# Fewer rows in the software stores of one chunk: two constants in a kernel that the DMA engines bound

## The chip, the cores and the metric

The kernel runs on one core of a Trainium2 chip. The metric is the device time of an execution in microseconds (us); each quoted time is a median over several executions. Before and changed kernel are compared on the same chip in alternating rounds. "Span" is the time from the first to the last recorded instruction of one profiled execution; it is 1.3 to 1.8 us shorter than the device time of the same execution.

## The reference

```python
# x: [16, 2048, 256] float32, W: [256, 256], lora_A: [256, 16], lora_B: [16, 256], lora_E: [16]
x_flat = x.reshape(-1, in_dim)                       # 32768 x 256
y = x_flat @ W
lora_out = ((x_flat @ lora_A) * lora_E) @ lora_B
y = y + scale * lora_out                             # back to [16, 2048, 256], float32
```

Input and output are 33.5 MB each, and all of it has to go through the DMA engines once.

## The kernel before

The 32,768 rows are cut into 4 chunks, each 128 partitions x 64 rows x 1 KB. A chunk is loaded into one of three buffers ("homes"), computed in place, and stored from there. For each group of four rows of all partitions GpSimd casts to bf16, TensorE transposes, VectorE copies back, TensorE multiplies with one merged weight, and ScalarE writes the result over the input. The order of the loads ("L") and stores ("S") of the hardware queue, as (chunk, first row, end row):

```python
ORDER = [
    ("A",), ("L", 0, 0, 16), ...          # cut: the other loads of chunks 0 to 2
    ("S", 0, 0, 40), ("S", 0, 40, 64),
    ("L", 3, 0, 32), ("L", 3, 32, 64),
    ("S", 1, 0, 64),
    ("S", 2, 2, 62),
    ("S", 3, 0, 64),
]
SHARED = 2
END_ROWS = 2
SHARES = (slice(108, 113), slice(0, 108), slice(113, P))
```

Of chunk 2 the hardware queue stores rows 2 to 61. GpSimd stores rows 0, 1, 62 and 63 with three software DMAs, one for each slice of the partitions:

```python
def share(engine, p, landed):
    def ends_of(rows):
        return rows[p].rearrange("p (q b) k -> p q b k", b=END_ROWS)[:, :: ROWS // END_ROWS - 1, :, :]
    engine.dma_start(out=ends_of(y_chunks[SHARED]), in_=ends_of(home(SHARED))).then_inc(landed, 16)

# GpSimd, after its last cast:
gpsimd.wait_ge(s_turned, N_GROUPS - NS + 1)
gpsimd.drain().then_inc(s_stage[N_GROUPS % UNROLL], 1)
gpsimd.wait_ge(s_shared, 1)
for p in SHARES:
    share(gpsimd, p, shared_stored)

# the hardware queue's engine, after its last issue:
sync.wait_ge(shared_stored, 16 * len(SHARES))
...                                        # cut: closing steps, then a wait for the last hardware stores
```

Of the kernel before, what the change touches and what calls it, by code (L numbers as in the profile page):

```python
# [27 lines left out]
    ("L", 3, 0, 32),  # L28
    ("L", 3, 32, 64),
    ("S", 1, 0, 64),  # L30
    ("S", 2, 2, 62),
    ("S", 3, 0, 64),
]

SHARED = 2
END_ROWS = 2
SHARES = (slice(108, 113), slice(0, 108), slice(113, P))

HELD = (2, 0)
# [18 lines left out]
def kernel(  # L58
# [105 lines left out]
# [4 lines that stand above are left out]
# [177 lines left out]
```

## Time and profile before

| | before |
|---|---|
| time, median of 6 executions | 161.32 us (161.14 to 161.55) |
| span of the profiled execution | 159.8 us |
| bytes moved | 67.43 MB, 422 GB/s over the span |
| busiest compute engine | PE, 60% |
| wait for the software stores over | 154.9 us |

How to read it: the prediction below shows the lines for the bound (the queues' share of sixteen engines), the stages and the queue's waits. Here is only the chain of work that ended last in the kernel before, by line, as a share of the span:

```profile
DMA out_dram<-home 28%; PE psum_y L269 25%; PE psum_xt L258 14%; DMA home<-in_x_dram 5%; POOL stage L200 1%; ACT home L221 1%; PE psum_y L291 1%; SPq L147 0%; ACTq L225 0%
```

PE (TensorE) stands in this chain with 40%, though it is not the bound: the chain ends with the issue of the last store, which waits for the last group. When that store is issued, at 122.4 us, the hardware queue still has some 16 us of chunks 1 and 2 ahead of it, so an earlier end of the compute should have moved nothing. A chain tells what released what; whether the queue in front of it was empty has to be read from the DMA share.

### The profile page before, as it was taken

What the parts mean: (1) busy time and instruction counts of PE and PEld (TensorE: products, weight loads), DVE (VectorE), ACT (ScalarE), POOL (GpSimd) and SP (SyncE); (2) the same over time, 40 slices, a digit from 0 to 9 for tenths busy, and PEclk for the clock granted to TensorE, in tenths of its full rate; (3) what the DMA queues carried; (4) which work ended last, traced back from release to release, by engine and by line L of the source; (5) the groups of instructions that cost most, each with busy time, mean ns of one, the idle gap of its engine ahead of it and who ended that gap; (6) DMA issues with size and microseconds to landing.
All of it is one profiled execution on the core that took longest, in us unless ns stands there. A gap on an engine that the chain in (4) does not pass through costs nothing.

```text
span 159.8 us, 2074 instructions
## 1 busy us (share of the span) xinstructions
PE 96.1 (60%) x782; PEld 84.2 (53%) x782; DVE 45.4 (28%) x66; ACT 66.1 (41%) x65; POOL 69.3 (43%) x73
## 2 busy tenths in 40 slices
PE   2769999999999900000999999999993000000000
PEld 1246899999999900000799999999992000000000
DVE  0113355555555500000155555555550000000000
ACT  3001477777777720000267777777775000000000
POOL 1072577777787300002577777778762000000000
PEclk9999999999999995555599999999999555555555
DMA  7999999999979997989999999998998997989976
GB/s 271 427 455 431 400 453 443 476 394 402 583 328 525 410 377 328 468 359 441 406 482 402 435 468 402 509 443 377 492 434 355 481 486 306 545 345 480 491 312 263
DMA packets 2451, 67.43 MB, mean 422 GB/s; under 512 B 512, under 2 KB 528, under 8 KB 784
## 3 DMA queue, kind: packets, MB, share of 16 engines
q1 hardware_dynamic: 2016, 66.60, 97.4%
q0 software_dynamic: 224, 0.52, 0.9%
q10 hardware_dynamic: 208, 0.28, 0.6%
q14 instruction: 3, 0.02, 0.0%
HBM read 33.85 MB, written 33.55 MB: 422 GB/s over the span
## 4 chain that ended last, share of the span: by engine, by line
PE 40%; DMA 33%; POOL 1%; ACT 1%; issue 0%; SPq 0%; ACTq 0%
DMA out_dram<-home 28%; PE psum_y L269 25%; PE psum_xt L258 14%; DMA home<-in_x_dram 5%; POOL stage L200 1%; ACT home L221 1%; PE psum_y L291 1%; SPq L147 0%; ACTq L225 0%
## 5 line engine op out<-in xcount | busy, mean ns | idle before, releaser
L200 POOL CAST stage<-home 128x1024 bf16<-128x1024 f32 x64 | 66.6, 1042 | 48.2 <-PE psum_xt L258 21.7
L221 ACT COPY home<-psum_y 128x1024 f32<-128x1024 f32 x64 | 64.8, 1012 | 54.3 <-PE psum_y L269 54.3
L269 PE MATMUL psum_y<-weff,xt 128*128 128x256 bf16 x512 | 69.0, 280 | 0.0
L242 DVE COPY xt<-psum_xt 128x1024 bf16<-128x1024 bf16 x64 | 44.3, 691 | 65.8 <-PE psum_xt L258 65.8
L258 PE MATMUL psum_xt<-ident,stage 128*128 128x128 f32 x260 | 41.9, 286 | 22.3 <-POOL stage L200 22.3
L269 PEld LDWEIGHTS psum_y<-weff,xt 128*128 128x128 bf16 x512 | 51.4, 100 | 6.2
L258 PEld LDWEIGHTS psum_xt<-ident,stage 128*128 128x128 f32 x260 | 32.3, 148 | 24.9 <-issue 23.7
L282 PE MATMUL psum_y<-ident 128*128 128x512 f32 x4 | 3.8, 1100 | 2.9 <-POOL ident L180 2.9
L282 PEld LDWEIGHTS psum_y<-ident 128*128 128x128 f32 x4 | 1.2, 323 | 3.9 <-POOL ident L180 2.9
L230 DVE TENSOR_SCALAR ate<-psum_y,e_sb 16x256 f32<-16x256 f32 x1 | 0.5, 472 | 7.2 <-DMA e_sb<-in_lora_E_dram 7.2
L168 POOL DMA_DIRECT2D out_dram<-home x3 | 2.0, 675 | 1.0 <-PE psum_xt L258 1.0
L221 ACT ACT_TABLE_LOAD x1 | 1.3, 1283 | 2.1 <-SPq L304 2.1
L291 PE MATMUL psum_y<-b_sb,ate 16*128 16x256 f32 x4 | 2.1, 666 | 0.0
L291 PEld LDWEIGHTS psum_y<-b_sb,ate 16*128 16x128 f32 x4 | 1.2, 318 | 0.5 <-issue 0.3
L246 DVE TENSOR_TENSOR weff<-w_sb,psum_y 128x512 bf16<-128x512 f32 x1 | 0.7, 687 | 1.4 <-PE psum_y L291 1.4
L178 POOL MEMSET ident<- 128x128 f32 x1 | 0.2, 205 | 1.7 <-SPq L304 1.7
L285 PEld LDWEIGHTS psum_y<-ident,a_sb 128*16 128x16 f32 x2 | 0.3, 137 | 1.2 <-issue 1.2
L285 PE MATMUL psum_y<-ident,a_sb 128*16 128x128 f32 x2 | 0.6, 421 | 0.0
L180 POOL TENSOR_SCALAR_AFFINE_SELECT ident<-ident 128x128 f32<-128x128 f32 x1 | 0.3, 283 | 0.2 <-POOL ident L178 0.2
L326 POOL MEMSET const-float32-0.0<- 128x1 f32 x1 | 0.1, 93 | 0.2 <-issue 0.2
L326 POOL MEMSET const-bfloat16-1.0<- 128x1 bf16 x1 | 0.1, 96 | 0.0
L326 POOL MEMSET const-uint8-127<- 128x1 uint8 x1 | 0.1, 96 | 0.0
(1 smaller groups left out, 0.1 us busy)
## 6 DMA issues: line engine op xcount, KB each, us to landing
home<-in_x_dram SPq DMA_DIRECT2D x4, 4096.0 KB, 24.4
out_dram<-home SPq DMA_DIRECT2D x1, 7680.0 KB, 38.2
home<-in_x_dram SPq DMA_DIRECT2D x2, 3072.0 KB, 16.7
out_dram<-home SPq DMA_DIRECT2D x1, 5120.0 KB, 45.2
out_dram<-home SPq DMA_DIRECT2D x1, 3072.0 KB, 44.7
home<-in_x_dram SPq DMA_DIRECT2D x1, 2048.0 KB, 7.6
out_dram<-home POOLq DMA_DIRECT2D x1, 432.0 KB, 30.2
w_sb<-in_W_dram ACTq DMA_DIRECT2D x1, 256.0 KB, 2.8
```

The costliest lines, as they stand in the source:

```text
L168: engine.dma_start(out=ends_of(y_chunks[SHARED]), in_=ends_of(home(SHARED))).then_inc(landed, 16)
L200: gpsimd.tensor_copy(out=stage[g % NS][:], in_=home(c)[:, b:b + CG, :]).then_inc(s_stage[g % UNROLL], 1)
L221: scalar.copy(out=home(c)[:, b:b + CG, :], in_=psum_y[g % NY][:]).then_inc(s_free[(g + NY) % UNROLL], 1)
L230: vector.tensor_scalar(out=ate[:], in0=psum_y[0][:R, :KT, :P], scalar1=e_sb[:], scalar2=float(scale), op0=ALU.mult, op1=ALU.mult,).then_in ...
L242: vector.tensor_copy(out=xt[g % NX][:], in_=psum_xt[g % NT][:].bitcast(BF16)).then_inc(s_xt[g % UNROLL], 1)
L246: vector.tensor_add(out=weff[:], in0=w_sb[:], in1=psum_y[1][:, :KT, :]).then_inc(s_free[0], 1)
L258: ins = tensor.transpose(psum_xt[i % NT][:, b, :], words[:, b, :], ident[:])
L269: ins = tensor.matmul(psum_y[i % NY][:, b, :], xt[i % NX][:, b, t::KT], weff[:, t, :], start=(t == 0), stop=(t == KT - 1),)
L282: tensor.matmul(psum_y[1][:, :2, :], ident[:], ident[:, None, :].to_broadcast([P, 4, P]), start=True, stop=True)
L285: ins = tensor.transpose(psum_y[0][:R, t, :P], a_sb[:, t, :], ident[:])
L291: ins = tensor.matmul(psum_y[1][:, t, :], ate[:, t, :], b_sb[:], start=True, stop=True)
L326: nc = _bacc.Bacc("TRN2", target_bir_lowering=False, num_devices=1)
```

## The change

The intent is to give less work to the software stores: one row at either end of chunk 2 in place of two, and the rows between to the hardware store. The whole diff:

```diff
-    ("S", 2, 2, 62),
+    ("S", 2, 1, 63),
     ("S", 3, 0, 64),
 ]
 
 SHARED = 2
-END_ROWS = 2
+END_ROWS = 1
```

The title under which the change was handed over also names straight code and drains (the prediction refers to it); they are not in the diff.

## The prediction

> **What bounds the kernel now.** I read the page first: the engines' busy shares, the forty slices, the DMA queues and the chain that ended last.
>
> ```profile
> PE 96.1 (60%) x782; PEld 84.2 (53%) x782; DVE 45.4 (28%) x66; ACT 66.1 (41%) x65; POOL 69.3 (43%) x73
> ...
> PE   2769999999999900000999999999993000000000
> ...
> DMA  7999999999979997989999999998998997989976
> ...
> DMA packets 2451, 67.43 MB, mean 422 GB/s; under 512 B 512, under 2 KB 528, under 8 KB 784
> ...
> q1 hardware_dynamic: 2016, 66.60, 97.4%
> q0 software_dynamic: 224, 0.52, 0.9%
> q10 hardware_dynamic: 208, 0.28, 0.6%
> ```
>
> No compute engine is busy over 60% of the span, and PE is empty in the last nine slices. The 16 DMA engines are full nearly throughout: the packets of queues q1, q0 and q10 take 97.4 + 0.9 + 0.6 = 98.9% of sixteen engines' span. So the bound is the packet time of the DMA engines. The software stores that the change is about are q0: 0.52 MB.
>
> Next, the stages. The columns are length, then busy time of PE, PEld, DVE, ACT and POOL, granted clock, DMA share, GB/s:
>
> ```profile
> 100.00:122.00 22.00, 21.32 (x196) 19.59 (x193) 10.59 (x16) 16.93 (x18) 16.17 (x17) 1.00 1.02 441
> 122.00:135.00 13.00, 0.00 (x0) 0.00 (x0) 0.00 (x0) 0.37 (x1) 0.00 (x0) 0.58 1.03 443
> 135.00:150.00 15.00, 0.00 (x0) 0.00 (x0) 0.00 (x0) 0.00 (x0) 0.00 (x0) 0.50 1.01 435
> 150.00:158.50 8.50, 0.00 (x0) 0.00 (x0) 0.00 (x0) 0.00 (x0) 0.00 (x0) 0.50 0.88 377
> 158.50:159.80 1.30, 0.00 (x0) 0.00 (x0) 0.00 (x0) 0.00 (x0) 0.00 (x0) 0.50 0.01 0
> ```
>
> From 122 us on only stores run, at 435 to 443 GB/s with every engine full; the last engines drain between 158.5 and 159.4 us. The end is therefore the end of whichever DMA engine has the longest list of packets. Last, the queue's own waits, the issues, and the instruction that follows the wait for the software stores:
>
> ```profile
> SPq L147 <- DMA out_dram<-home: 32.1, 1, 32.1
> ...
> out_dram<-home SPq DMA_DIRECT2D x1, 7680.0 KB, 38.2
> ...
> out_dram<-home POOLq DMA_DIRECT2D x1, 432.0 KB, 30.2
> ...
> out_dram<-home POOLq DMA_DIRECT2D x1, 60.0 KB, 34.8
> ...
> out_dram<-home POOLq DMA_DIRECT2D x1, 20.0 KB, 9.5
> ...
> L147 SPq COMPARE_BRANCH  x1: 33/33/33, 154.9 to 154.9; - x1
> ```
>
> The wait for the software stores is over by 154.9 us, more than 4 us before the end. They take the engines' time but their completion does not hold the end. They are 20 + 432 + 60 = 512 KB for 5 + 108 + 15 = 128 partitions: 4 KB each, 2 KB at either end.
>
> **Engine by engine.** No view prints the engine of a packet, but the trace has every packet's start, duration, size and queue, and on a full engine the next packet begins within about 4 ns of the last one's end. Matching ends to starts from 112 us on gives 16 lists. Twelve have 10 software packets of 4,096 B; four have 2 each, and in the other 8 turns an 8 B dummy of 9 ns. (At one place two lists run together, and which one holds a 539 ns packet is my choice: I give it to the list that would otherwise have only one.) Durations, from these records: 65,536 B 2,418 ns; 61,440 B (chunk 2's store) 2,267 ns; 4,096 B 159 ns; 2,048 B (the load of W) 84 ns; 1,024 B 46 ns. Per KB it is (2,418 - 2,267) / 4 = 38 ns. The lists end, in us:
>
> - the twelve: 158.46, 158.57, 158.64, 158.70, 158.71, 158.81, 158.81, 158.82, 158.98, 159.02, 159.02, 159.03
> - the four: 158.65, 158.97, 159.08, 159.39
>
> So the uneven shares are a balance: at 113 us the four were behind the twelve (their packets begin at 112.97 to 113.58, those of the twelve at 112.20 to 112.76), and 8 x (159 - 9) = 1,200 ns less work lets them almost catch up. Almost: one of the four still ends last.
>
> **What the Trainium skill says.** "DMA: Bandwidth & Descriptors", section "Queues, rings and completion order": each DMA engine takes turns between its rings, a packet at a time. The trace agrees: a 159 ns software packet follows each 2,267 ns packet of the store on twelve engines. The same page, "Why a DMA increments its semaphore by 16 and not by 1": the number of engines is the largest up to 16 that divides the outer size, and software DMAs take consecutive engines from a rotating cursor. 5, 108 and 15 partitions would give 5, 12 and 15 engines, leaving 11 + 4 x 9 + 1 = 48 dummies; the trace has 48 packets of 8 B. The same page, "Issuing engines are not separate DMA queues": DMAs of all issuers share the same 16 engines; the 98.9% above agrees, so moving rows between the queues adds no bandwidth. The same page, "Specifications": runs of 512 B or more go at line rate; the new runs of 1 KB are above that, but no store here has 1 KB runs to check it.
>
> **The change part by part.** The diff alters two constants; what the title says of straight code and drains is nowhere in it, so I take those as unchanged. Compute, loads, waits, dummies and the number of DMAs stay. The store of chunk 2 waits for group (128 + 63 - 1) // 4 = 47, and before for (128 + 62 - 1) // 4 = 47: the same. Total bytes are the same.
>
> 1. Chunk 2's hardware store grows from 60 to 62 rows. Each engine has 8 such packets, each 2 KB longer: +8 x 2 x 38 = about +600 ns on all 16.
> 2. A software packet falls from 2 x 2 KB to 2 x 1 KB, 159 to 84 ns by the load's packet: -10 x 75 = -750 ns on the twelve, -2 x 75 = -150 ns on the four.
> 3. Sum: the twelve -150 ns, the four +450 ns. In bytes, the twelve go from 520 to 516 KB of chunk 2 and the four from 488 to 500 KB: the balance is half undone.
>
> All of it lies on full engines, so it moves the ends one for one: the twelve to 158.3-158.9, the four to 159.1-159.8. The last engine is one of the four both times, so the span grows by 0.45 us, from 159.8 to about 160.2. Without the odd 539 ns packet the four ended by 159.08, again later than every one of the twelve, and the step would be the same.
>
> **The rivals.** (a) The twelve set the end in ordinary executions, and the four are ahead: then the change gains at most 0.15 us. Against it: the average end of the four is 159.02, of the twelve 158.80. For it: the gap is only 0.2 us, and the lag of the four comes from longer packets that need not fall alike in each execution. (b) Packets with 1 KB runs don't get shorter (cost by the run, not the byte): all 16 engines then gain 600 ns and the time rises by about 0.6 us. The 1,024 B loads at 46 ns speak against it, but they are loads. (c) The software stores' completion matters: halving them would bring a gain. Against it: the 4 us of slack. No change from this. (d) The store that begins at row 1, not row 2, writes at a worse alignment, and its packets lengthen. 128 packets over 16 engines are 18 us per engine, so 3% would be 0.5 us. Nothing speaks for it; both starts are whole KB.
>
> **Range and chances.** I add not the full 0.45 but 0.35 us, as (a) has perhaps one chance in four: 161.5 + 0.35 = 161.85. The runs of before spread by 0.37 us, and (a) to (d) span -0.15 to +1.0; 161.2 to 162.5 should hold it 8 times in 10. Two per cent is 3.2 us, several times any term here: within 2% at 0.98, 0.01 for either side.
>
> **What would show each step.** Packets of 63,488 B at about 2,342 ns and software packets of 2,048 B at about 84 ns show steps 1 and 2; 159 ns would be rival (b), over 2,400 ns rival (d). The 16 lists should separate: twelve ending near 158.6, four near 159.4 on average, the last near 159.8. Equal ends, or the twelve last, would be rival (a). In the stages, the share in the last 1.3 us should rise a little, and the software wait should end as early as before. The prediction fails if the load phase, 100 us earlier, shifts the engines against one another by more than 0.5 us from run to run, or if the software DMAs land on other engines.

## The result, and the profile after

The changed kernel takes **161.56 us** (161.48 to 161.77, 6 runs), before 161.32 us in the same rounds: ratio 1.0015, 95% interval 1.0002 to 1.0028. A second set on another occasion gave 161.56 against 161.16 us, ratio 1.0023 (1.0009 to 1.0037). A ratio is the mean time of one kernel's fast runs over that of the other's in the same rounds, so not quite the ratio of the medians. So the change costs 0.2 to 0.4 us, about 0.2%; the forecast was +0.35 us, written as 161.85 because it started from an earlier median of 161.5.

The profile of the changed kernel, the slices of DMA and the queues:

```profile
DMA  7999999999969987989999999997997998989974
...
DMA packets 2387, 67.43 MB, mean 421 GB/s; under 512 B 496, under 2 KB 512, under 8 KB 720
...
q1 hardware_dynamic: 2016, 66.86, 97.6%
q10 hardware_dynamic: 208, 0.28, 0.6%
q0 software_dynamic: 160, 0.26, 0.4%
```

The software bytes are halved, 0.52 to 0.26 MB, and the hardware queue took them over, 66.60 to 66.86 MB. The two shares sum to 98.0% in place of 98.3% of a span that is 0.4 us longer: the engines work as much as before, and a little more of the span is left over. The software queue has 160 packets, not 224: 80 with data (48 of 4,096 B and 32 of 2,048 B) in place of 128. The prediction had not foreseen that. The issues of the changed kernel:

```profile
out_dram<-home SPq DMA_DIRECT2D x1, 7936.0 KB, 37.5
...
out_dram<-home POOLq DMA_DIRECT2D x1, 216.0 KB, 21.5
...
out_dram<-home POOLq DMA_DIRECT2D x1, 30.0 KB, 25.7
...
out_dram<-home POOLq DMA_DIRECT2D x1, 10.0 KB, 9.8
```

And the instruction that follows the wait for the software stores:

```profile
L147 SPq COMPARE_BRANCH  x1: 33/33/33, 147.3 to 147.3; - x1
```

The software stores land sooner (the large one in 21.5 us in place of 30.2), and their wait is over at 147.3 us in place of 154.9. It gained 7.6 us and the time gained nothing: that wait was hidden before and is hidden after. The stages of the changed kernel, in the columns of the prediction:

```profile
122.00:135.00 13.00, 0.82 (x8) 0.49 (x5) 0.00 (x0) 1.57 (x2) 0.17 (x1) 0.69 1.07 463
135.00:150.00 15.00, 0.00 (x0) 0.00 (x0) 0.00 (x0) 0.00 (x0) 0.00 (x0) 0.50 1.00 431
150.00:158.50 8.50, 0.00 (x0) 0.00 (x0) 0.00 (x0) 0.00 (x0) 0.00 (x0) 0.50 0.87 378
158.50:160.20 1.70, 0.00 (x0) 0.00 (x0) 0.00 (x0) 0.00 (x0) 0.00 (x0) 0.50 0.00 0
```

A view of stages cannot resolve 0.4 us: a packet is counted where it starts, so the shares run over 1 at one edge and fall short at the other. What resolves it are the packet records, matched into one list for each engine as the prediction tells. In the following table "slow" sums, over all sixteen engines from 136 us on, what packets took beyond the usual duration of their size (those over by more than 15 ns); these sums need no matching.

```
                     before   before, again   changed   changed, again
end of the last       159.39        159.63     159.72        159.64
mean end, all 16      158.85        159.08     158.89        158.84
mean end, the four    159.02        159.37     159.20        159.06
mean end, the twelve  158.80        158.99     158.80        158.77
slow, us (packets)    2.4 (20)      2.9 (19)   0.2 (1)       0.2 (1)
```

In both traces of before, lists cross near 151.6 us (in the second also near 139 us), so which list is whose is a choice there. The means are those of the matching with the fewest unusual gaps: every list keeps its usual overlap of 3 to 4 ns, and one of the four waits 100 ns (112 in the second trace) before one slow software packet. By it the last list is one of the four in both traces of before, as in both of the change.

The four engines with few software packets were to end 0.45 us later on average. They did not: the averages of two traces are 159.20 us before and 159.13 in the changed kernel. The slow packets are the difference. Before, they sat mostly on the four (2.0 of 2.4 us, and 2.7 of 2.9 in the second trace: 0.59 us an engine), and in the changed kernel they are gone, but for one: +0.45 - 0.59 + 0.05 = -0.09 us, where -0.07 was measured.

### The profile page after: what moved, and what is told of

It is laid out like the page before. It is cut to its first block, busy times and chain, and to the rows that moved or that the text cites. A ratio compares the mean times of both kernels' runs of the same rounds, so it can differ in the third digit from the quotient of the medians.

```text
span 160.2 us, 2074 instructions
## 1 busy us (share of the span) xinstructions
PE 94.9 (59%) x782; PEld 83.4 (52%) x782; DVE 45.4 (28%) x66; ACT 66.1 (41%) x65; POOL 68.9 (43%) x73
## 3 DMA queue, kind: packets, MB, share of 16 engines
q1 hardware_dynamic: 2016, 66.86, 97.6%
## 4 chain that ended last, share of the span: by engine, by line
PE 39%; DMA 35%; POOL 1%; ACT 1%; issue 0%; SPq 0%; ACTq 0%
DMA out_dram<-home 30%; PE psum_y L269 25%; PE psum_xt L258 14%; DMA home<-in_x_dram 5%; POOL stage L200 1%; ACT home L221 1%; PE psum_y L291 1%; SPq L147 0%; ACTq L225 0%
## 5 line engine op out<-in xcount | busy, mean ns | idle before, releaser
L258 PE MATMUL psum_xt<-ident,stage 128*128 128x128 f32 x260 | 41.4, 283 | 25.1 <-POOL stage L200 25.0
L291 PE MATMUL psum_y<-b_sb,ate 16*128 16x256 f32 x4 | 1.1, 405 | 0.0
L291 PEld LDWEIGHTS psum_y<-b_sb,ate 16*128 16x128 f32 x4 | 0.7, 184 | 0.2 <-issue 0.2
## 6 DMA issues: line engine op xcount, KB each, us to landing
out_dram<-home POOLq DMA_DIRECT2D x1, 216.0 KB, 21.5
```

What stands on the lines that cost most here:

```text
L258: ins = tensor.transpose(psum_xt[i % NT][:, b, :], words[:, b, :], ident[:])
L291: ins = tensor.matmul(psum_y[1][:, t, :], ate[:, t, :], b_sb[:], start=True, stop=True)
```

## The experiments

The theory: sixteen full DMA engines, of which four are late by the end of the loads; the uneven software shares spare them; the change takes half of that away. The rivals: the twelve other engines set the end; or the software stores, or their runs of 1 KB, are a cost in themselves. All times are medians of 5 runs, but for before_again.

| run | time | before, same rounds | ratio (95%) |
|---|---|---|---|
| all_hw | 161.88 | 161.16 | 1.0042 (1.0027 to 1.0056) |
| half_alone (wrong result on purpose) | 160.87 | 161.16 | 0.9975 (0.9961 to 0.9990) |
| after_again | 161.56 | 161.16 | 1.0023 (1.0009 to 1.0037) |
| four_rows | 164.49 | 161.16 | 1.0198 (1.0183 to 1.0213) |
| spare_last | 162.25 | 161.31 | 1.0061 (1.0047 to 1.0075) |
| even_sw | 161.88 | 161.31 | 1.0039 (1.0026 to 1.0053) |
| top_two | 161.89 | 161.31 | 1.0037 (1.0023 to 1.0051) |
| top_six | 162.19 | 161.31 | 1.0060 (1.0045 to 1.0074) |
| early_one | 161.52 | 161.25 | 1.0014 (1.0001 to 1.0028) |
| early_two | 161.87 | 161.25 | 1.0038 (1.0025 to 1.0052) |
| early_four | 167.96 | 161.25 | 1.0417 (1.0402 to 1.0432) |
| before_again (one run, state unknown) | 161.31 | 161.25 | none |

### No software stores: all_hw

```diff
-    ("S", 2, 2, 62),
+    ("S", 2, 0, 64),
-        sync.wait_ge(shared_stored, 16 * len(SHARES))      (and GpSimd's three stores removed)
```

> Chunk 2 is stored by the hardware queue alone (rows 0 to 63), no software stores. Theory (the end is that of four late DMA engines, which the uneven software shares spare): the twelve lose 10 software packets of 159 ns and gain 8 x 4 KB x 37.7 = 1,206 ns, -0.38 us; the four gain 1,206 ns less 2 x 159 and 8 dummies of 9 ns, +0.82 us. The four end near 159.9, the last of them 160.2 us after the span's start; time about 0.8 us over before (near 162.1). Rival (the twelve set the end, or the software stores are a cost in themselves): the time falls by 0.3 us or more.

It took 0.7 us more (161.88 against 161.16), as the theory said to 0.1 us. Every engine now has the same bytes; three lists end at 159.10, 159.34 and 160.05, the other thirteen by 158.86. So the time agrees, but not the picture behind it: the theory had all four late engines near 159.9, and only one gets there. The slow packets, which the theory left out, are gone here too (0.0 us from 136 us on). The software stores still earn their keep, and not by bandwidth: they save 0.7 us, and even_sw below shows that this comes from their being uneven.

### The other four engines: spare_last

```diff
-SHARES = (slice(108, 113), slice(0, 108), slice(113, P))
+SHARES = (slice(0, 108), slice(108, 113), slice(113, P))
```

> Two rows at either end as before, but the 108-partition share goes first, so that other four engines are spared[...]. Theory (it is those four that are late): they now carry 10 software packets in place of 2, +8 x 150 = +1.2 us, and end near 160.2 or later; time about 1.0 us over before (near 162.4). Rival (any four would do; the lag follows from having fewer software packets): no difference from before.

0.9 us more, as expected. The same bytes, packets and DMAs, and only the order of three issues is different. In its trace the four lists that are late at 113 us (first packets at 113.4 to 113.9) now hold 10 software packets and end at 159.77, 160.08, 160.12 and 160.46, and the four lists with nine dummies at 158.12 to 158.40. This is the cleanest proof: **which** engines are spared decides, not how much software work there is.

### The same packets, evenly: even_sw

```diff
-SHARES = (slice(108, 113), slice(0, 108), slice(113, P))
+SHARES = (slice(0, P),)
```

> Two rows at either end by software, in one DMA of 128 partitions: 8 software packets of 4 KB on every engine, 512 KB of chunk 2 each, as without software stores. Theory (only the balance matters): like all_hw, the four +0.9 us, time about 0.8 us over before. Rival (what matters is how much the software stores take from the hardware queue): like before.

0.6 us more, near the theory's 0.8 and far from "like before". The software queue carries the same 0.52 MB as before:

```profile
q1 hardware_dynamic: 2016, 66.60, 96.9%
q0 software_dynamic: 144, 0.52, 0.8%
```

With the bytes of the two queues unchanged and the balance gone, the loss is that of all_hw within noise (ratios 1.0039 and 1.0042).

### One part of the change alone: half_alone, beside after_again

```diff
-END_ROWS = 2
+END_ROWS = 1          (the hardware store stays at rows 2 to 61: rows 1 and 62 are not stored)
```

> Part 2 of the change alone: software stores of one row at either end, but the hardware store stays at rows 2 to 61, so rows 1 and 62 of each partition of chunk 2 are never stored and the result is wrong on purpose. Theory: the twelve lose 0.79 us each, the four only 0.15 us, and as the four set the end the time falls by about 0.15 us, to about 161.2, with the twelve ending near 158.0 in the trace. Rival (the twelve set the end): the time falls by 0.4 us or more, as 0.25 MB less is stored.

> The change once more, beside its part alone and for a second trace. Theory: 0.2 to 0.4 us over before, and about 0.6 us over half_alone (the hardware packets' 8 x 2 KB on every engine). In the trace the four engines with dummies end last on average, by 0.4 us or more over the mean of the twelve. Rival (the first result was the slow packets of one profile and noise): no difference from before.

The change itself repeated: +0.4 us. Of its trace, "0.4 us or more over the twelve" was missed: the four end at 159.06 on average, the twelve at 158.77, 0.3 apart (0.4 in the first trace of the change). Between the two kernels, 161.56 - 160.87 = 0.69 us is what the hardware packets' 8 x 2 KB cost, near the theory's 0.6. But half_alone alone gained 0.29 us (by the means 0.40, interval 0.16 to 0.63), where the theory said 0.15: a miss, between theory and rival; the time alone does not rule out the rival's 0.4. The ends do. In its trace the last engine ends at 159.04 and the twelve by 158.47, so the twelve do not set the end, and the rival falls too. But the slow packets are gone, 0.2 us in one packet against 2.4 in 20. Halving the software stores relieves the four of more than their two software packets.

The other part alone (longer hardware packets, software stores as before) can't be run: two queues would write the same rows in no order.

### The other way: four_rows

```diff
-    ("S", 2, 2, 62),
+    ("S", 2, 4, 60),
-END_ROWS = 2
+END_ROWS = 4
```

> The other way: four rows at either end by software, hardware rows 4 to 59. In bytes of chunk 2: the twelve 528 KB (+8, +0.3 us), the four 464 KB (-24, -0.9 us). Theory: now the twelve set the end, near 159.1 to 159.3, with the four at 158.1 to 158.5; time 0 to 0.3 us over before. Rival (fewer bytes on the hardware queue is what helps, whichever engines): the time falls by as much as one row rises it, 0.25 us.

It took 3.3 us more, and both sides missed it. In four_rows, the queue's waits are:

```profile
SPq L156 <- DMA out_dram<-home: 38.2, 1, 38.2
SPq L147 <- DMA out_dram<-home: 37.5, 1, 37.5
```

and the instruction that follows the wait for the software stores (the second of the two lines above):

```profile
L147 SPq COMPARE_BRANCH  x1: 33/33/33, 161.4 to 161.4; - x1
```

The wait now ends at 161.4 us, after the last hardware packet (159.66). The last software packet ends at 161.07. A software packet of 4 KB gets one turn for each hardware packet of about 2.3 us, so twenty of them do not fit beside what is left of chunks 1, 2 and 3. The counts in the lists agree, but no run isolates this: early_four below was to test it and failed. And the closing steps, which before ran beside the last hardware store, now follow that wait: the span goes on for 1.7 us after it, to 163.1, where before it ended 0.4 us after the last packet. So with four rows a wait that was hidden has become the end. Part of the lateness is again slow packets: from 136 us on they sum to 6.5 us, in 21 packets.

### One run in place of two: top_two and top_six

```diff
-    ("S", 2, 2, 62),
+    ("S", 2, 2, 64),                               (top_six: 6, 64, and END_ROWS = 6)
         def ends_of(rows):
-            return rows[p].rearrange("p (q b) k -> p q b k", b=END_ROWS)[:, :: ROWS // END_ROWS - 1, :, :]
+            return rows[p][:, 0:END_ROWS, :]
```

> The bytes of the change (two rows of each partition by software) as one run of 2 KB at the start, rows 0 and 1, and the hardware store rows 2 to 63. Theory (bytes for each engine decide): as the change, 0.2 to 0.4 us over before. Rival (the number of 1 KB runs, or the alignment of the long packets, costs): different from the change by 0.2 us or more, and other durations for the software packets.

> A candidate for better than both: rows 0 to 5 of each partition by software in one run of 6 KB (before: 4 KB, the change: 2 KB), hardware rows 6 to 63. The twelve 524 KB (+4, +0.15 us), the four 476 KB (-12, -0.45 us). Theory: the ends of the two groups meet near 158.9 to 159.2; time from 0.2 us under before to the same. Rival (more software work costs in itself, or runs over 4 KB are cut and cost more): slower than before.

Both expectations rested on engine counts that did not hold. top_two took 0.6 us more than before, by its ratio (1.0037) as much as even_sw and all_hw (1.0039 and 1.0042). Its lists show the reason: five engines carry 9 partitions' software bytes, ten carry 8, one carries 3 (5 x 9 + 10 x 8 + 3 = 128). As one run for each partition, the DMAs of 5, 108 and 15 partitions are laid over the engines in equal portions of 1, 7 and 1 partitions, all from the same engine on, and no longer on 5, 12 and 15. The four late engines are among those with 9. So it is one more kernel without the balance, and of run length it says only this: a 2 KB packet took 84 ns as one run here and 84 ns as two runs of 1 KB in the changed kernel. top_six has the same spread (nine, eight and three partitions an engine) and also the most slow packets (9.7 us from 136 us on); which of the two costs its 0.9 us is not separated. It does not beat before.

### A second trace, and the software stores earlier: before_again, early_two, early_one, early_four

```diff
-    ("S", 1, 0, 64),
-    ("S", 2, 2, 62),
+    ("S", 1, 2, 62),                               (early_one: 1, 63; early_four: 4, 60)
+    ("S", 2, 0, 64),
-SHARED = 2
+SHARED = 1
             gpsimd.tensor_copy(...)
+            if g == 48:                            (and the three stores removed from the end)
+                gpsimd.wait_ge(s_shared, 1)
+                for p in SHARES:
+                    share(gpsimd, p, shared_stored)
```

> The kernel before once more, for a second trace. Theory: again the four engines with dummies end last on average, by 0.1 to 0.3 us, and their packets from 139 us on are slow in sum by 0.2 to 0.9 us each, as in the first trace, while in both traces of the change they were not (0 to 0.2 us). Rival (the slow packets were chance): no such packets this time, and the four end earlier.

> The software stores carry two rows at either end of chunk 1 in place of chunk 2, issued after group 48 (near 97 us, some 20 us earlier), so that they are over before chunk 3's store. Same bytes on each engine as before. Theory (balance, plus slow packets where software packets run beside chunk 3's store): as before, or up to 0.3 us faster, as the slow packets on the four go. Rival (the software stores slow whatever runs beside them by the same): as before.

> The same with one row at either end: the change, but early. Bytes alone make the four 0.45 us later than in early_two. Theory (the smaller measured effect of the change, about 0.3 us, is 0.45 less the slow packets that it removes): 0.4 to 0.5 us over early_two. Rival (the four do not quite set the end): 0.3 us or less over early_two.

> The same with four rows at either end, to find why four_rows took 3.3 us more. There the twelve had 20 software packets, one to each turn of about 2.3 us, and the wait for the software stores ended at 161.4, after the last hardware packet. Theory (that wait became the end): issued 20 us earlier it is over by about 145 us, and the time falls back to 0 to 0.4 us over before. Rival (four rows of software packets cost in themselves): stays 2 us or more over before.

before_again says that the slow packets belong to the kernel and were not chance: 2.9 us in 19 packets, of them 0.56, 0.19, 0.99 and 0.99 us on the four engines with dummies. The four end 0.4 us after the twelve on average, where 0.1 to 0.3 was expected.

The three early kernels failed by a mistake of the edit. GpSimd's drain, which releases TensorE for the last group, now comes after the software stores in place of before them. The drain of early_four:

```profile
L207 POOLq DRAIN  x1: 22021/22021/22021, 120.1 to 120.1; - x1
```

and among the waits of the same kernel the last turn of TensorE that waited for it:

```profile
PE psum_xt L259 <- POOLq L207: 20.0, 1, 20.0
```

In the kernel before it is:

```profile
L203 POOLq DRAIN  x1: 34/34/34, 117.9 to 117.9; - x1
```

The drain took 22.0 us and ended at 142.1, just after the last software packet of early_four (141.6). In early_two it took 16.0 us, in early_one 6.3. The last group and the store of chunk 3 then came late, and the DMA engines ran empty, as the stage of early_four from 141.6 to 146.5 us shows (the columns are those of the prediction's stages; DMA share and GB/s are zero):

```profile
141.60:146.50 4.90, 2.79 (x12) 1.91 (x12) 0.00 (x0) 1.01 (x1) 0.00 (x0) 0.50 0.00 0
```

So early_four and early_two test nothing of the theory. early_one came out 0.35 us under early_two, where 0.4 to 0.5 over was expected; with early_two held up by its drain, this difference says nothing of the bytes. early_one is sound on its own: its drain was over at 126 us and chunk 3's store was issued at 130.3, while the queue still had chunk 2. It took 0.27 us more than before, like the change, with no slow packet from 136 us on. early_two does show that the slow packets are not tied to chunk 3's store: 1.8 us of them fell between 120 and 136 us. Whether two early rows behind a drain in the right place would beat before is open.

## Why the prediction was right

**The bound and the end.** Right: even_sw and spare_last moved the time by 0.6 and 0.9 us with the bytes of both queues unchanged and only the balance between engines different. One reading was too strong: a 159 ns software packet does not follow each 2,267 ns packet on the twelve, but five of the eight; 8 B and 4 B packets take two of the other turns.

**Step 1, the longer hardware packets.** Right: all 128 are of 63,488 B, and their median is 2,342 ns, as predicted. after_again less half_alone is 0.69 us against 0.60.

**Step 2, the shorter software packets.** Right in sum, wrong in kind. I expected ten packets of 2,048 B on each of the twelve. There are four of 4,096 and two of 2,048 B: software runs of two partitions share a packet up to 4 KB. In time it is 10 x 159 - (4 x 159 + 2 x 84) = 786 ns, where I had 750. Rival (b), cost by the run, would have left the packets as long as before: it falls.

**Step 3, the sum.** The twelve: expected -0.15 us, measured -0.11 (158.89 to 158.78, each the average of two traces, which differ by up to 0.2 us). The four: expected +0.45, measured -0.07 in the mean of their ends. **The term that was mis-sized** is this one: it took all packets but the named ones as unchanged. The spared engines of before have slow packets, 0.59 us on each, and the change removes them; on average that takes back all that the change costs the four. What remains is that the last engine is later.

**Which engine is last.** Not the four alike. In every trace (but those of the early kernels, which move other packets then) one engine has eight hardware packets in a row of 2,554 to 2,596 ns between 100 and 120 us, in place of 2,418 (1.2 us of delay). In both traces of the change, in all_hw, half_alone, spare_last, even_sw and top_two the list that ends last is that engine's (159.72, 159.64, 160.05, 159.04, 160.46, 159.97, 159.93). In the traces of before it ended at 158.97 and 159.38, and another list ended last, at 159.39 and 159.63. This engine has only 0.2 us of slow packets from 136 us on, before and in the change alike, so the prediction's sum should hold for it, and it does. Against its mean in before it ends 0.5 us later in the change (theory 0.45), 0.1 earlier in half_alone (0.15), and later by 0.9 in all_hw (0.8), 0.8 in even_sw (0.9) and 1.3 in spare_last (1.2). The other three of the four have 0.72 us of slow packets each in before and none in the change: 0.45 - 0.72 = -0.27 us, and they end 0.26 us earlier (159.20 to 158.95). So the one engine becomes the last, and the end of the kernel moves by less than it does, as a slowed neighbour was last before: by 0.0 to 0.3 us in these traces, 0.2 to 0.4 in the timed runs.

**Rival (a)**, for which I took 0.10 off: it fails. The twelve do not set the end of the changed kernel in either trace, and by the matching above not that of before. The deduction was about right in size, for a reason that I had not named: that the forecast came so near was in this part luck.

**Rivals (c) and (d).** No effect, as predicted: the wait for the software stores gained 7.6 us and nothing came of it, and the packets of the shifted store have the predicted length. But four_rows shows how near (c) was: at twice the rows it is the end.

**Open:** why the spared engines get slow packets. They come with the uneven two-row, the four-row and the six-row stores, and not with the one-row stores, nor with two rows spread evenly (even_sw, 0.2 us) or in one run (top_two, 0.2 us). Nor are they on spared engines alone: in spare_last these have 1.1 of 2.2 us, and in top_six no four are spared. No run shows what the engine waits for in them. Why four engines are late at 113 us, and one of them once more, is open too.

## What to carry to other kernels

When all DMA engines are full, ask which of them ends last; a total of bytes or a share of busy time cannot tell. A small uneven DMA can level them, and then its size and the order of its issues are tuned values: here half as much cost 0.2%, none 0.4%, the wrong order 0.6%, twice as much 2%. A hidden wait stays hidden only as long as its packets find enough turns beside the others'.

## What the Trainium skill lacked or had wrong

- "DMA: Bandwidth & Descriptors", section "Why a DMA increments its semaphore by 16 and not by 1", says that software DMAs give "some direct copies" sixteen engines with equal portions, rounded up, and does not say which. Here DMAs of 5, 108 and 15 partitions with two separate runs for each partition went to 5, 12 and 15 engines (by the 48 dummies of 8 B in before), and with one run for each partition to all in portions of 1, 7 and 1 (9, 8 and 3 partitions an engine in top_two).
- The same page, section "SWDGE vs HWDGE vs iDMA", has packets of up to 4,096 B "preferably". The two-run stores agree (two partitions of 2 KB in one packet of 4,096 B, 159 ns), but a single run of 6 KB went as one packet of 6,144 B (234 ns), and the packets of the hardware queue, of which that passage does not speak, were up to 65,536 B (2,418 ns). So turns between queues were as coarse as 2.4 us, which by the lists is part of what made four_rows late.
- "Perfetto Trace Analysis", section "Sequencer-only Instruction (DRAIN, etc)", names only the sequencer and the semaphore as actors. A GpSimd drain behind software stores took 6.3, 16.0 and 22.0 us in the three early kernels, in each until 0.6 to 0.7 us after the last software packet, against 34 ns ahead of them.
- No page has the slow packets beside an uneven software DMA: 2.4 and 2.9 us in 20 and 19 packets from 136 us on in the two traces of before, 2.0 and 2.7 us of it on the engines that it leaves free (by the matching above), and 0.2 us in one packet in both of the change.
